# Forget gate as 16 more columns of the first keys' products, with later first heads and last pieces

## The chip, the cores and the metric

The kernel runs on one core of a Trainium2 chip. The metric is the device time of one execution in microseconds; three executions of the kernel before took 2311.81, 2313.56 and 2315.46 us, with a median of 2313.56 us.

The core has five engines that run side by side and wait for one another by semaphores: TensorE (PE, matrix products into PSUM), VectorE (DVE), ScalarE (ACT), GpSimd (POOL) and SyncE (SP). SP and POOL issue the transfers between HBM and the on-chip memory here. Each engine works through its own instructions in a fixed order.

## What is computed

Two decoder layers, D = 2048, 256 positions, float32. Layer 0 mixes with a gated MLP over positions and a linear recurrence, layer 1 with forgetting attention; after each comes a gated MLP with a short convolution. The change lies in the attention, `mixer_c`:

```python
def mixer_c(h, w_in, b_f, q_gain, k_gain, w_out):
    q, k, v, g, f = jnp.split(h @ w_in, [D_MODEL, 2 * D_MODEL, 3 * D_MODEL, 4 * D_MODEL], axis=-1)
    q = rms_norm(q.reshape(shp), q_gain)         # 16 heads of 128
    k = rms_norm(k.reshape(shp), k_gain)
    log_f = jax.nn.log_sigmoid(f + b_f)          # the forget gate: 16 columns, one for each head
    c = jnp.cumsum(log_f, axis=1).transpose(0, 2, 1)
    ...
        s = jnp.einsum('bthd,bshd->bhts', q[:, lo:hi], k[:, :hi]) * scale
        s = s + c[:, :, lo:hi, None] - c[:, :, None, :hi]
        p = jax.nn.softmax(jnp.where(causal, s, -jnp.inf), axis=-1)
    ...
    return (o * jax.nn.sigmoid(g)) @ w_out
```

The forget gate is a projection of the normed input onto only 16 columns, followed by a log-sigmoid and a running sum over the positions.

## The kernel before

Every projection is computed in float32 as three products of rounded parts. Activations and weights are split into a high part, rounded to the matrix engine's type (`ah`, `wh`), and the rest (`al`, `wl`); the products are `ah*wh + ah*wl + al*wh`. `weights()` does this for weights: SP loads a tile `w` from HBM (L156, four buffers), ACT casts it to `wh` (L162, three buffers), DVE subtracts to get `wl` (L165, three buffers), and PE multiplies. The three engines and SP form a pipeline that runs ahead of PE as far as the buffers allow.

`project_tok` (L194) computes one group of 512 columns (four heads) for all 256 positions. It runs over the 16 blocks of 128 rows of the weights (k = 0 to 15), two of them in each tile of 128x1024 (512 KB): a chunk. The two halves of the positions (T = 0, 1) have one PSUM bank each (the pool `pm`). Each chunk has 12 products of 512 columns (L225 to L227), each group 96. The norm's factor for a position is multiplied in when the bank is emptied, as the scale `Rt[:, T]` of an ACT instruction (L816).

In `mixer_c` the groups of heads are g = 0 to 3, each with queries Q, keys K and values V. Q0 and K0, those of the first group, are projected first (`early`); then the norm's finish makes the factors both for positions on partitions (`Rt`) and, by a product with a matrix of ones (`finish`, L353), for positions along the columns (`R`). Then for each group: Q and K are emptied, normed by head (L305, L306, L824), transposed in blocks of 32x32 by DVE (L250), and put in place by 16 copies from on-chip memory to on-chip memory (L255), eight of them issued by SP and eight by POOL. The results are the `turn` tiles. For g = 0 the forget gate stands ahead of V0's projection.

`forget()` (L728) projects with `w_cf`, whose 16 columns are padded to 128: two loads of 512 KB on SP and, for each k, one product of 512 columns with the high part of the weights stationary (L186: high and low part of the activations) and one of 256 with the low part (L189). The gate's columns end up on 128 partitions, positions along the columns. ACT and DVE fold the parts, multiply by `R`, add the bias and compute the log-sigmoid (L734 to L738), DVE scans over the positions (L739), and POOL writes the 16 rows to HBM (`cd`) and reads them back spread over all partitions (`cb`, 2 MB). `columns()` (L745) transposes `fc` on PE for the other direction (L748).

`attend(h, ...)` (L755) is one head's attention, written as a generator. `tick()` advances the generators in flight at every chunk, so that their pieces come between the chunks of later projections; at each `yield` a generator waits for the next `tick()`. Its first step casts the turned queries and keys to `qk` with their gains (L758); the next one computes the scores (L761, L762). `depth[0]` is how many generators run at a time, here two.

`add_four` (L367) and, in the `ffn` stage, `add_y` bring an output projection's piece q = 0 to 3 into the residual `x`: copy, transpose, 16 copies, then after `LAG` steps (one fewer for the last piece) four additions (L378) and the next norm's input; after the last piece and `WAIT` more steps comes the norm's `finish_tok`. `project_four` (L231, products L242 to L244) is the projection with weights from four blocks, used for the attention's gate, the output projections and the `ffn`.

The order of the instructions of each engine is set when the program is built: the program's order gives priorities, from which a scheduler places each engine's instructions, and generators interleave as said above. SP and POOL issue their transfers in their own order; each can be held up by a wait of the transfer at its head.

## Time and profile before

| What | Value |
|---|---|
| median of three runs | 2313.56 us |
| the runs | 2311.81, 2313.56, 2315.46 us |
| profiled execution, first to last instruction | 2312.9 us |
| mean granted clock of TensorE in it | 0.999 |
| PE busy | 2300.0 us, 99% |
| DVE busy | 1559.5 us, 67% |
| ACT busy | 1307.0 us, 57% |
| POOL busy | 350.4 us, 15% |
| DMA | 481.44 MB, 208 GB/s mean |

A row of the timeline reads: start in us from the beginning of the span, duration in us, engine, source line, operation, output and inputs by their names, shapes, number of instructions in the row, and in brackets the idle time of the engine ahead of it with what ended it. "SPq" and "POOL ... DMA_DIRECT2D" are the issues of transfers: their time is that of issuing, not that of the data. Durations of PE's products overlap, since the engine is pipelined: what a product costs is read from the distance between two starts. A row of the waits reads: the engine and the line that waited, the engine and the line that it waited for, microseconds in total, how often, the longest. A row of the groups reads: line, engine, operation, names, number | busy us, mean ns of one | idle us ahead of them, by releaser.

### The profile page before, as it was taken

How to read it: one execution, taken by the hardware profiler on the slowest of the kernel's cores; microseconds unless marked ns; L12 is line 12 of the kernel's file. 1: busy time of each engine (PE TensorE's matmuls, PEld its weight loads, DVE VectorE, ACT ScalarE, POOL GpSimd, SP SyncE). 2: the span in 40 equal slices, each digit the busy share in tenths (PEclk: the TensorE clock that was granted, in tenths of full speed). 3: DMA queues.
4: the chain of work that ended last, by engine and by line, in shares of the span. 5: the costliest groups of instructions: out<-in, count | busy, mean ns of one | idle time of the engine just before them, and what ended most of it. 6: DMA issues, size and time to landing. Idle time of an engine off the chain costs nothing.

```text
span 2312.9 us, 31358 instructions
## 1 busy us (share of the span) xinstructions
PE 2300.0 (99%) x10354; PEld 1904.7 (82%) x10354; DVE 1559.5 (67%) x2345; ACT 1307.0 (57%) x1958; POOL 350.4 (15%) x650
## 2 busy tenths in 40 slices
PE   9999999999999999999999999999999999999998
PEld 7888888888888888888888888887888888888887
DVE  7677866776566657766866665666776476667766
ACT  7567655665555546654565556655655465455642
POOL 0100112122012002111211101111221022012102
PEclk9999999999999999999999999999999999999999
DMA  8655577777677767776666655777777677667765
GB/s 274 204 161 173 175 218 220 235 235 212 208 210 207 217 196 212 223 216 186 197 230 194 190 182 178 225 221 227 225 219 216 192 218 209 210 205 213 222 206 166
DMA packets 497748, 481.44 MB, mean 208 GB/s; under 512 B 116288, under 2 KB 468688, under 8 KB 497456
## 3 DMA queue, kind: packets, MB, share of 16 engines
q1 hardware_dynamic: 475488, 453.08, 63.9%
q0 software_dynamic: 20944, 24.04, 4.5%
q10 hardware_dynamic: 1152, 2.31, 0.3%
q8 instruction: 81, 1.33, 0.3%
q14 instruction: 83, 0.68, 0.1%
HBM read 435.24 MB, written 2.11 MB: 189 GB/s over the span
## 4 chain that ended last, share of the span: by engine, by line
PE 95%; DVE 1%; DMA 1%; ACT 1%; issue 1%; POOL 0%; SPq 0%; ACTq 0%; DVEq 0%
PE pm L243 26%; PE pm L244 26%; PE pm L242 26%; PE pm L226 5%; PE pm L227 5%; PE pm L225 5%; DVE wl L165 1%; ACT wh L162 0%; PE px L593 0%; DMA w<-in_w_up 0%; PE pm L186 0%; DMA w<-in_w_v 0%; PE px L762 0%; DMA turn<-tmp 0%; PE px L784 0%
## 5 line engine op out<-in xcount | busy, mean ns | idle before, releaser
L165 DVE TENSOR_TENSOR wl<-w,wh 128x1024 fp32r<-128x1024 f32 (+1 forms) x820 | 998.5, 1220 | 647.2 <-ACT wh L162 639.1
L162 ACT ACTIVATE wh<-w 128x1024 fp32r<-128x1024 f32 (+1 forms) x820 | 864.1, 1056 | 797.2 <-PE pm L244 574.4
L242 PE MATMUL pm<-wh,a 128*128 128x512 f32 x1792 | 699.5, 391 | 1.5 <-ACT wh L162 1.5
L243 PE MATMUL pm<-wl,a 128*128 128x512 f32 x1792 | 699.1, 390 | 1.1 <-DVE wl L165 1.1
L244 PE MATMUL pm<-wh,a 128*128 128x512 f32 x1792 | 698.3, 390 | 0.0
L255 POOL DMA_DIRECT2D zt<-tmp x416 | 225.3, 550 | 1206.8 <-DVE tmp L250 1034.6
L243 PEld LDWEIGHTS pm<-wl,a 128*128 128x128 f32 x1792 | 337.0, 188 | 71.8 <-DVE wl L165 2.7
L242 PEld LDWEIGHTS pm<-wh,a 128*128 128x128 f32 x1792 | 336.7, 188 | 71.2 <-ACT wh L162 1.9
L244 PEld LDWEIGHTS pm<-wh,a 128*128 128x128 f32 x1792 | 336.9, 188 | 69.7
L242 PE MATMUL pm<-wh,hid 128*128 128x512 f32 x688 | 267.6, 389 | 0.0
L243 PE MATMUL pm<-wl,hid 128*128 128x512 f32 x688 | 267.6, 389 | 0.0
L244 PE MATMUL pm<-wh,hid 128*128 128x512 f32 x688 | 267.6, 389 | 0.0
L255 POOL DMA_DIRECT2D turn<-tmp x224 | 121.5, 550 | 739.5 <-DVE tmp L250 332.5
L225 PE MATMUL pm<-wh,a 128*128 128x512 f32 x504 | 199.2, 395 | 0.3 <-ACT wh L162 0.3
L226 PE MATMUL pm<-wl,a 128*128 128x512 f32 x504 | 196.5, 390 | 1.5 <-DVE wl L165 1.5
L227 PE MATMUL pm<-wh,a 128*128 128x512 f32 x504 | 196.5, 390 | 0.0
L244 PEld LDWEIGHTS pm<-wh,hid 128*128 128x128 f32 x688 | 129.1, 188 | 26.9
L243 PEld LDWEIGHTS pm<-wl,hid 128*128 128x128 f32 x688 | 129.1, 188 | 26.8
L242 PEld LDWEIGHTS pm<-wh,hid 128*128 128x128 f32 x688 | 129.1, 188 | 26.8
L226 PEld LDWEIGHTS pm<-wl,a 128*128 128x128 f32 x504 | 94.7, 188 | 21.3 <-DVE wl L165 2.1
L225 PEld LDWEIGHTS pm<-wh,a 128*128 128x128 f32 x504 | 94.7, 188 | 20.0 <-ACT wh L162 1.0
L227 PEld LDWEIGHTS pm<-wh,a 128*128 128x128 f32 x504 | 94.7, 188 | 19.8
(214 smaller groups left out, 1828.7 us busy)
## 6 DMA issues: line engine op xcount, KB each, us to landing
w<-in_w_up SPq DMA_DIRECT2D x352, 512.0 KB, 4.6
w<-in_w_dn SPq DMA_DIRECT2D x176, 512.0 KB, 4.5
w<-in_w_cqkv SPq DMA_DIRECT2D x96, 512.0 KB, 4.4
w<-in_w_abo SPq DMA_DIRECT2D x32, 512.0 KB, 4.8
w<-in_w_cg SPq DMA_DIRECT2D x32, 512.0 KB, 4.4
w<-in_w_co SPq DMA_DIRECT2D x32, 512.0 KB, 4.7
zt<-tmp SPq DMA_DIRECT2D x416, 32.0 KB, 2.8
zt<-tmp POOLq DMA_DIRECT2D x416, 32.0 KB, 2.6
```

What stands on the lines that cost most here:

```text
L162: deep["act"] = SC.activation(wh[:, p], w[:, p], AF.Copy)
L165: V.tensor_tensor(wl[:, p], w[:, p], wh[:, p].bitcast(F32), ALU.subtract)
L225: PE.matmul(ps[T], ah, h, start=k + i == 0, stop=False)
L226: PE.matmul(ps[T], ah, l, start=False, stop=False)
L227: PE.matmul(ps[T], al, h, start=False, stop=k + i == KT - 1)
L242: PE.matmul(ps[T], ah, h, start=k + i == 0, stop=False)
L243: PE.matmul(ps[T], ah, l, start=False, stop=False)
L244: deep['mm'] = PE.matmul(ps[T], al, h, start=False, stop=k + i == n - 1)
L255: (nc.sync, nc.gpsimd)[(a + b) % 2].dma_start(dst[BLK * b:BLK * (b + 1), :, a * n:(a + 1) * n], tmp[BLK * a:BLK * (a + 1), b * 4 * n:(b + ...
```

## The change

`w_cf`'s 16 columns go into K0's projection. For each k one tile of 528 columns is put together from two loads: 16 columns of `w_cf` (128 rows of 64 bytes, 8 KB, issued by POOL) and 512 columns of K's weights (256 KB, issued by SP). It is cast and split as one tile. Each of the 96 former products is two: one of 272 columns (the gate's 16 and K0's first 256) into a bank of the pool `px`, one of 256 columns into a bank of `pm`. K0's emptying takes four instructions for that reason.

The padded projection with its 1 MB of loads, the fold, and the factor `R` with its product are gone. `forget()` comes after K0's transposes in the program and ahead of V0's projection; it empties the 16 columns scaled by `Rt` (`ft`), transposes them on PE (two products into one bank), and goes on with 16 partitions in place of 128. `columns()` transposes 16 partitions in place of 128.

Three constants change. `STAND` is new: the first two heads of every group wait three steps more ahead of their first instruction. `LAST` = 5 replaces `LAG - 1` = 3 for the last piece of `add_four` and `add_y`; `WAIT` goes from 4 to 2. Helpers that are no longer called are removed.

The instructions in the order of each engine, before and after: PE 10021 and 10088 rows, DVE 2250 and 2250, ACT 1807 and 1811, POOL 94 and 110, SP 914 and 920. Around the end of K0 the order in the changed kernel is:

- SP: K0's sixteen loads, Q0's eight copies, V0's first six loads (chunks 0 to 5), K0's eight copies. Before, two loads of `w_cf` and V0's first two loads stood ahead of Q0's copies.
- POOL: sixteen loads of `w_cf`, Q0's eight copies, `cd`, `cb`, K0's eight copies. Before: Q0's, K0's, `cd`, `cb`.
- ACT: the casts of K0's last tiles, the emptying of K0 and the gate, two `qk` casts of queries, the gate's Abs, the cast of V0's first tile, the gate's Exp and Ln with the head norm's between, the next casts of V0.
- PE: K0's last product, the two transposes of the gate, V0's first chunk; the transposes of `columns()` in V0's third chunk.

With `LAST` and `WAIT` the order of every engine at the ends of the first three stages stays as it was; the very last addition of the program moves.

```diff
 LAG = 4
-WAIT = 4
+LAST = 5
+WAIT = 2
+STAND = 3
...
-        early = project_tok(w_cqkv[0], norm), project_tok(w_cqkv[CH // 4], norm)
+        first = project_tok(w_cqkv[0], norm)
+        pa, pb = [bank() for _ in range(2)], [pm.tile([P, 512], F32, tag="pm", name=nm("pm")) for _ in range(2)]
+        n = CH + 512
+        for k in range(KT):
+            if k % 2 == 0:
+                tick()
+            w = wp.tile([P, n], F32, tag="w", name=nm("w"), bufs=4)
+            wh = wp.tile([P, n], F32R, tag="wh", name=nm("wh"), bufs=3)
+            wl = wp.tile([P, n], F32R, tag="wl", name=nm("wl"), bufs=3)
+            nc.gpsimd.dma_start(w[:, 0:CH], w_cf[:, k * P:k * P + CH])
+            nc.sync.dma_start(w[:, CH:n], w_cqkv[CH // 4][:, k * 512:(k + 1) * 512])
+            deep["act"] = SC.activation(wh, w, AF.Copy)
+            V.tensor_tensor(wl, w, wh.bitcast(F32), ALU.subtract)
+            a = norm.a[k]
+            for T in range(2):
+                ah, al = a[:, T * P:(T + 1) * P], a[:, S + T * P:S + (T + 1) * P]
+                for j, (a_, t) in enumerate(((ah, wh), (ah, wl), (al, wh))):
+                    start, stop = k + j == 0, k == KT - 1 and j == 2
+                    PE.matmul(pa[T][:, 0:CH + S], a_, t[:, 0:CH + S], start=start, stop=stop)
+                    PE.matmul(pb[T][:, 0:S], a_, t[:, CH + S:n], start=start, stop=stop)
         drain()
         depth[0] = 2
-        R, Rt = norm.finish(), norm.Rt
+        Rt = norm.Rt
...
         def forget():
-            f = project_norm(w_cf, A, R, hp.tile([P, S], F32, tag="f", name="f"))
+            f = hp.tile([P, S], F32, tag="f", name="f")[0:CH]
+            ft = hp.tile([P, 2, LANE], F32, tag="ft", name="ft")
+            ps = bank()
+            for T in range(2):
+                SC.activation(ft[:, T, 0:CH], pa[T][:, 0:CH], AF.Copy, scale=Rt[:, T:T + 1])
+                PE.transpose(ps[0:CH, T * P:(T + 1) * P], ft[:, T, 0:CH], ident)
...
-            V.tensor_scalar(f, f, pp[:, C_BF:C_BF + 1], None, ALU.add)
+            V.tensor_scalar(f, ps[0:CH, 0:S], pp[0:CH, C_BF:C_BF + 1], None, ALU.add)
...
         def columns(fc):
             ps = bank()
             for T in range(2):
-                PE.transpose(ps[:, T * P:(T + 1) * P], fc[:, T * P:(T + 1) * P], ident)
+                PE.transpose(ps[:, T * CH:(T + 1) * CH], fc[:, T * P:(T + 1) * P], ident[0:CH, 0:CH])
...
         def attend(h, q, k, v, o):
             d0 = (h % 4) * P
+            for _ in range(STAND if h % 4 < 2 else 0):
+                yield
...
             for j in range(3):
-                if g == 0 and j == 2:
-                    fc = forget()
-                ps = early[j] if g == 0 and j < 2 else project_tok(w_cqkv[j * (CH // 4) + g], norm)
+                ps = None if g == 0 and j == 1 else first if g + j == 0 else \
+                    project_tok(w_cqkv[j * (CH // 4) + g], norm)
                 z = piece("z", 2) if j < 2 else piece("v", 2)
                 for T in range(2):
-                    SC.activation(z[:, T], ps[T], AF.Copy, scale=Rt[:, T:T + 1])
+                    if ps is None:
+                        SC.activation(z[:, T, 0:S], pa[T][:, CH:CH + S], AF.Copy, scale=Rt[:, T:T + 1])
+                        SC.activation(z[:, T, S:512], pb[T][:, 0:S], AF.Copy, scale=Rt[:, T:T + 1])
+                    else:
+                        SC.activation(z[:, T], ps[T], AF.Copy, scale=Rt[:, T:T + 1])
...
                 qkv.append(z)
+                if g == 0 and j == 1:
+                    fc = forget()
...
     def add_four(q, ps, z, tmp, dst, nxt):
...
-            for _ in range(LAG - (q == 3)):
+            for _ in range(LAST if q == 3 else LAG):
                 yield
...
         def add_y(q, finish):
...
-                for _ in range(LAG - (q == 3)):
+                for _ in range(LAST if q == 3 else LAG):
                     yield
```

More of the change, by code (lines that the diff above doesn't have):

```diff
@@ L257, in transposed @@
                                   .rearrange("p (m r) -> p m r", m=4))
-    def fold(ps):
-        t = tp.tile([P, S], F32, tag="ev", name=nm("ev"), bufs=3)
-        SC.activation(t, ps[:, S:2 * S], AF.Copy)
-        V.tensor_tensor(t, ps[:, 0:S], t, ALU.add)
-        return t
-    def project_norm(wsrc, acts, R, out=None, run=2):
-        t = fold(project(wsrc, acts, run=run))
-        if out is None:
-            out = t
-        V.tensor_tensor(out, t, R, ALU.mult)
-        return out
     def split(dst, src, gain=None, eng=SC, turn=False):
@@ L349, in finish_tok @@
             self.Rt = Rt
-        def finish(self, tok=False):
-            ps = bank()
-            PE.matmul(ps[:, 0:S], ones, self.acc, start=True, stop=True)
-            R = cp.tile([P, S], F32, tag="R", name=nm("R"), bufs=2)
-            rsq(R, ps[:, 0:S], D)
-            if not tok:
-                return R
-            for _ in self.finish_tok():
-                pass
-            return R, self.Rt
-    def add_x(m, ps):
-        t = tp.tile([P, S], F32, tag="ev", name=nm("ev"), bufs=3)
-        SC.activation(t, ps[:, S:2 * S], AF.Copy)
-        V.tensor_tensor(xT[m], xT[m], ps[:, 0:S], ALU.add)
-        V.tensor_tensor(xT[m], xT[m], t, ALU.add)
     def add_four(q, ps, z, tmp, dst, nxt):
@@ L740, in forget @@
             cd = dp.tile([CH, S], F32, tag="cd", name="cd")
-            nc.gpsimd.dma_start(cd, fc[0:CH, :])
+            nc.gpsimd.dma_start(cd, fc)
             nc.gpsimd.dma_start(cb, cd.partition_broadcast(P))
```

10 lines of the change are left out of this document (5 added, 5 removed).

## The prediction

> **What bounds the kernel now.** I read the page first: the span, the busy shares, the chain of work that ended last.
>
> ```profile
> span 2312.9 us, 31358 instructions
> PE 2300.0 (99%) x10354; PEld 1904.7 (82%) x10354; DVE 1559.5 (67%) x2345; ACT 1307.0 (57%) x1958; POOL 350.4 (15%) x650
> PE 95%; DVE 1%; DMA 1%; ACT 1%; issue 1%; POOL 0%; SPq 0%; ACTq 0%; DVEq 0%
> ```
>
> PE is 95% of the chain. A change can therefore save time in two ways only: fewer or shorter products, or less waiting by PE. It can lose by making PE wait. The table of waits for PE says how little waiting there is:
>
> ```profile
> PE pm L226 <- DVE wl L165: 1.5, 2, 0.8
> PE pm L242 <- ACT wh L162: 1.5, 1, 1.5
> ```
>
> Then the timeline of PE at the place that the change touches: the end of K0 (the first keys), R's product, the forget gate, the start of V0.
>
> ```profile
> 1155.88 0.39 PE L227 MATMUL pm<-wh,a 128*128 128x512 f32 x1
> 1156.10 0.59 PE L353 MATMUL px<-acc,ones 128*128 128x256 f32 x2
> ...
> 1157.25 0.62 PE L186 MATMUL pm<-a,wh 128*128 128x512 f32 x2
> 1157.94 0.63 PE L186 MATMUL pm<-a,wh 128*128 128x512 f32 x2
> ...
> 1162.12 0.40 PE L225 MATMUL pm<-wh,a 128*128 128x512 f32 x1
> ```
>
> K0 ends at 1156.10 and V0 starts at 1162.12 with no idle time marked between. Those 6.02 us are PE work that the change takes out. What else they do is seen on SP's queue and on ACT in the same stretch:
>
> ```profile
> 1142.87 2.78 SPq L156 DMA_DIRECT2D w<-in_w_cf  x2
> 1147.77 3.27 SPq L156 DMA_DIRECT2D w<-in_w_cqkv  x2
> 1151.97 5.37 SPq L255 DMA_DIRECT2D turn<-tmp  x8
> 1157.75 4.36 SPq L156 DMA_DIRECT2D w<-in_w_cqkv  x4
> ```
>
> The two loads at 1147.77 are V0's first, issued ahead of Q0's eight turned copies; the two `w_cf` loads stand ahead of them. So before the change, PE had the forget weights and two V loads in hand while SP spent 5.37 us on copies.
>
> **The change part by part.** *Forget products out, wider K0 products in.* R's product and the 16 + 16 forget products go: 1162.12 - 1156.10 = 6.02 us off PE. K0's 96 products of 512 columns become 96 of 272 and 96 of 256. A 512-column product costs 1156.10 - 1155.88 = 0.22, over longer runs 0.227 us. Two of 512 with two of 256 take 1157.94 - 1157.25 = 0.69, so one of 256 is (0.693 - 0.453) / 2 = 0.120. I take 0.127 for 272 (sixteen columns more at (0.227 - 0.120) / 256 each). Per old product: 0.127 + 0.120 - 0.227 = +0.020, times 96 = +1.9 us. Bounds: 0 if the split were free, +3 if the rows' rounding (0.01) falls against it. K0 then ends at E = 1156.1 + 1.9 = 1158.0. Of this sum the Trainium skill ("TensorE: Matmul & The Clock Gate", Back-to-back issue gap) has another price: a gap of N/2.4 + 2.5 ns, so a split costs about 9 ns and the 96 of them an estimated 0.9 us, a result 1 us lower; the rows' spacing of 227 ns for 512 columns is over its 216, and I go by the rows.
>
> *Transposes.* Two of the gate's 128x16 tiles are added behind K0; the two in V's third chunk shrink:
>
> ```profile
> 1183.91 0.38 PE L748 MATMUL px<-cst,fc 128*128 128x128 f32 x2
> ```
>
> About 0.2 us net; 0 to 0.5.
>
> *What stands ahead of V0 now.* Program order on SP becomes K0's sixteen 256 KB loads, Q0's eight copies, then V0's load: no load of V is ahead of the copies, and there is no PE work behind K0 to cover them. On ACT, between K0's evacuation and the cast of V0 (`wh`, L162), stand two `qk` casts (L758), which need all sixteen of Q0's copies, and the Abs of the gate (L735). Whatever holds `qk` holds these, and with V0's cast DVE's `wl` and all of PE. The sixteen `w_cf` loads on POOL wait for the same `w` buffers as SP's, so the last goes out near 1149.5, ahead of Q0's copies; they hold nothing up there. In before the two steps on ACT were:
>
> ```profile
> 1160.27 0.50 ACT L758 ACTIVATE qk<-turn,gq 128x256 f32<-128x256 f32 x1
> ...
> 1168.76 0.40 ACT L735 ACTIVATE fa<-f 128x256 f32<-128x256 f32 x1
> ...
> 1174.21 1.06 ACT L162 ACTIVATE wh<-w 128x1024 fp32r<-128x1024 f32 x1 [1.29 <-DMA w<-in_w_cqkv]
> ```
>
> DVE has Q0's transposes at 1150.60 and ends them at 1151.9:
>
> ```profile
> 1150.60 1.30 DVE L250 STREAM_TRANSPOSE tmp<-z 128x512 f32<-128x512 f32 x2
> ```
>
> Q0 itself is unchanged, so this stays near 1151.5. SP's copies then run 1151.6 to 1156.8 (5.2 us), and V0's load goes out at 1156.9. After K0's copies a load issued at 1170.37 was cast at 1174.21, 3.84 us later:
>
> ```profile
> 1165.15 5.11 SPq L255 DMA_DIRECT2D turn<-tmp  x8
> 1170.37 1.48 SPq L156 DMA_DIRECT2D w<-in_w_cqkv  x3
> ```
>
> So V0's `wh` starts at 1160.7 at the earliest, E + 2.7; with 1 us more for a later landing E + 3.7. Add the cast, 1.06: first V product at E + 3.8 to 4.8. The `wl` product behind it waits for DVE (L165), 0.8 as in the waits above, and after such a pause PE loses clock or waits once more: 1.4 us, worked out below. Together 6.0 to 7.0 us of loss behind E if nothing else is late.
>
> *POOL's pause.* POOL issues the other eight copies of each batch. In the timeline of POOL, a pause of some 2.1 to 2.4 us with the releaser "issue" recurs inside a batch:
>
> ```profile
> 858.77 0.55 POOL L255 DMA_DIRECT2D zt<-tmp  x1 [2.09 <-issue]
> ...
> 1152.56 4.33 POOL L255 DMA_DIRECT2D turn<-tmp  x8 [33.99 <-DMA w<-in_w_cqkv]
> ...
> 1223.11 4.37 POOL L255 DMA_DIRECT2D turn<-tmp  x8 [45.41 <-issue]
> ...
> 1585.33 1.63 POOL L255 DMA_DIRECT2D turn<-tmp  x3 [17.42 <-DVE tmp L250]
> 1589.35 2.71 POOL L255 DMA_DIRECT2D turn<-tmp  x5 [2.39 <-issue]
> ```
>
> The groups of POOL's DMAs between the pause at 858 and that at 1221, then between 1222 and 1588, give 89 + 16 + 1 + 1 = 107 and 107:
>
> ```profile
> L255 POOL DMA_DIRECT2D zt<-tmp x89 | 48.2, 550 | 213.7 <-DVE tmp L250 132.3 <-issue 81.4
> L255 POOL DMA_DIRECT2D turn<-tmp x16 | 8.7, 550 | 42.5 <-DMA w<-in_w_cqkv 34.0 <-DVE tmp L250 8.5
> L742 POOL DMA_DIRECT2D cb<-cd x1 | 0.6, 575 | 5.0 <-DMA cd<-fc 5.0
> L741 POOL DMA_DIRECT2D cd<-fc x1 | 0.5, 511 | 1.9 <-DVE fc L739 1.9
> ...
> L255 POOL DMA_DIRECT2D turn<-tmp x107 | 58.0, 550 | 351.2 <-DVE tmp L250 144.3 <-ACT wh L162 106.0 <-issue 100.9
> ```
>
> One DMA counts as one, small `cd` and large `cb` alike. The change puts sixteen more on POOL (one `w_cf` load of 8 KB for each k) ahead of Q0's copies. Before, Q0's and K0's sixteen copies, `cd` and `cb` lay between the count and the pause ahead of Q1's first copy; sixteen more DMAs bring that pause forward to about Q0's third copy (18 - 16 = 2 behind its first). The pause 107 further on moves from q = 3 of the output projection (fourth copy, 1589.35) to q = 1 of it.
>
> In before the pauses at Q1 and at q = 3 are where PE waited:
>
> ```profile
> 1235.47 0.50 PE L225 MATMUL pm<-wh,a 128*128 128x512 f32 x1 [0.29 <-ACT wh L162]
> 1236.73 0.50 PE L226 MATMUL pm<-wl,a 128*128 128x512 f32 x1 [0.76 <-DVE wl L165]
> ...
> 1599.59 0.39 PE L244 MATMUL pm<-wh,a 128*128 128x512 f32 x1
> 1601.45 0.50 PE L242 MATMUL pm<-wh,a 128*128 128x512 f32 x1 [1.48 <-ACT wh L162]
> 1602.71 0.50 PE L243 MATMUL pm<-wl,a 128*128 128x512 f32 x1 [0.76 <-DVE wl L165]
> ...
> 1604.01 0.63 PE L242 MATMUL pm<-wh,a 128*128 128x512 f32 x1
> ...
> 1607.00 0.55 PE L243 MATMUL pm<-wl,a 128*128 128x512 f32 x1
> ```
>
> At Q1 the step from L225 to L226 is 1.26 instead of 0.23, the wait ahead of it 0.29; with the edges 1.6 us. At q = 3 the step to 1601.45 is 1.86 instead of 0.23, the next 1.26 instead of 0.23, and from 1604.01 to 1607.00 seven steps take 2.99 instead of 1.59: 1.6 + 1.0 + 1.4, with the edges 4.4 us. The Trainium skill (the same page, Part 1) has the clock fall to half after an idle window of about 3.4 us; the rows show nearly twice the spacing after two gaps of 1.6 and 1.0, and by either a wait of 8 us here is followed by slow products.
>
> With the pause in Q0's copies POOL ends them late. Before, it began 0.59 behind SP (1152.56) and took 4.33; now it would begin at 1152.2 and end at 1152.2 + 4.33 + 2.4 = 1158.9. How long after that the copies are used: at most 3.4 us without a pause (1156.89 to the `qk` at 1160.27, which waited for no DMA); 6.05 at Q1 (1227.48 to the row below) and 5.6 at q = 3 (1592.06 to the row below), where SP's next loads ran at the same time:
>
> ```profile
> 1233.53 0.93 ACT L758 ACTIVATE qk<-turn,gq 128x256 f32<-128x256 f32 x2 [5.42 <-DMA w<-in_w_cqkv]
> ...
> 1597.70 1.10 DVE L378 TENSOR_TENSOR x<-x,turn 128x256 f32<-128x256 f32 x3 [3.53 <-DMA w<-in_w_up]
> ```
>
> V0's loads follow Q0's copies in the same way, so I go by the upper rows and take 5.2, a little less, since K0's last `w` buffers come free one by one: `qk` at 1164.1 = E + 6.1, bounds E + 4.3 and E + 6.95. Then 0.9 for two of them, 0.40 for the Abs, 1.06 for the cast: first V product at E + 8.4; `wl` 0.8 and clock 1.4 make it 10.6, bounds 8.8 and 11.5.
>
> *STAND, LAST, WAIT.* STAND moves the scores of a group's first two heads by three chunks; work of the same size, later, between products that are ready: 0, with -1 to +1 for a cover missed. LAST and WAIT leave the order of every engine at the three norm boundaries as it was and move only the very last addition: 0.
>
> *Sum*, against the profiled 2312.9: -6.0 + 1.9 + 0.2 + 10.6 - 1.6 (no pause in Q1) = +5.1, with nothing for the pause moved from q = 3 to q = 1, where the additions meet the same burst of loads (-4.4 to +0.6). Span 2318.0; the median of the runs, 2313.56, lies 0.66 above the profile, so 2318.7.
>
> **The rivals.**
>
> *No pause at Q0.* If what POOL counts is not DMAs (descriptors, instructions), the pause falls among the `w_cf` loads, 5 us ahead of need. Then only V0's load behind the copies is left: -6.0 + 1.9 + 0.2 + 6.5 - 1.6 = +1.0, about 2314.6, with 2313 to 2316. For: `w_cf` has 128 rows of 64 bytes, a shape that no row of before shows. Against: the two 107s with `cb` in one.
>
> *Covered.* V0's cast isn't held: the copies land in 2 us as their normal median, ACT takes `qk` before E, V0's first product comes within 2 us of E, and PE's two old waits vanish. -6.0 + 1.9 + 0.2 + 3 - 1.6 - 4.4 = -6.9, about 2306.7. For: before's `qk` at 1160.27 waited for no DMA, though SP's copies had ended at 1157.34. Against: SP's queue, where V0's load cannot pass the copies.
>
> *K0 starves.* Four buffers of one k hold half the prefetch of four of two: 4 x 6 x 0.247 = 5.9 us against 4 x 12 x 0.227 = 10.9, with two small DMAs per k, one on POOL with its 2 us pauses. If one k comes late, PE waits 1 to 4 us and the clock falls (1.4): 2 to 5 more, 2320 to 2324 along with the forecast's boundary. The Trainium skill ("DMA: Bandwidth & Descriptors", Specifications) speaks for it: rows under 512 B are slow, and these are 64 B; no row of before has one.
>
> *Edits without effect.* That LAST and WAIT do nothing is in the sum; 0 either way.
>
> **How the numbers follow.** Forecast 42% (2318.7, own range 2316 to 2321); no pause at Q0 27%; covered 18%; starved 13%. A change of 0.2%, 4.6 us, is about what a measurement tells from none. The forecast lies at +5.1, so part of it counts as the same; of the pause moved to q = 1 some fall to either side. Slower: 28 of the forecast's 42 and 12 of starved, 40%. Faster: the covered 18 and 6 of the others with q = 3's 4.4 us gone, 24%. Same 36%. The range 2307 to 2322 leaves out the far ends of covered and starved.
>
> **What would show it.** L353 and L186 gone, K0's products at 0.247 a pair. PE idle behind the last of them: `wh` of V0 waiting on `qk`, and `qk` on the turned copies; a POOL pause inside Q0's batch and none at Q1; products at twice the spacing after it. I am wrong if the gap on PE between K0 and V0 is under 5 us, if POOL's pause lies elsewhere, or if K0's products wait.

## The result and the profile after

| | before | after |
|---|---|---|
| median of six runs each, side by side | 2314.57 us (2311.81 to 2318.26) | 2325.18 us (2319.48 to 2329.15) |
| ratio of the two, 95% interval | | 1.0044 [1.0034, 1.0055] |
| profiled execution, span | 2312.9 us | 2327.3 us |

The changed kernel is slower by 10.6 us in the medians, where +5.1 was forecast; the time of 2318.7 is 6.5 us too low. The profiled execution of after is the slowest of its six runs (2329.15 us), so its trace shows more loss than the medians: 14.4 us of span.

The page of after begins like this: the span, the busy times, the shares of the chain that ended last.

```profile
span 2327.3 us, 31551 instructions
PE 2301.9 (99%) x10418; PEld 1907.1 (82%) x10418; DVE 1554.8 (67%) x2345; ACT 1306.5 (56%) x1965; POOL 358.8 (15%) x666
PE 93%; DMA 2%; DVE 1%; ACT 1%; issue 1%; SPq 0%; POOL 0%; ACTq 0%; DVEq 0%; POOLq 0%
```

PE's busy time is only 1.9 us higher, and its share of the chain fell from 95% to 93%: the loss is mostly waiting. The table of PE's waits (engine and line that waited, what it waited for, us in total, how often, the longest) says for what:

```profile
PE pm L227 <- ACT wh L164: 9.9, 2, 7.1
PE pm L228 <- DVE wl L167: 2.9, 3, 1.7
```

To see where each microsecond came in, I set the start of every product that both kernels have against its start in before. This lag grows or shrinks at the places in the table and is flat between them, but for short swings where `STAND` has moved pieces of heads:

| place in the profiled executions | change of the lag | forecast |
|---|---|---|
| ahead of the attention, at 33 and 460 us | +2.5 | none |
| K0, and on to the steady part of V0 | +6.7 | -6.0 + 1.9 + 0.2 + 10.6 = +6.7 |
| V0's seventh tile | +5.4 | no such term |
| rest of g = 0, small steps | -0.4 | 0 |
| Q1 | -1.4 | -1.6 |
| output projection, q = 1 and q = 3 | +6.35 and -4.4 | 0 together |

The sum is +14.75. The first line is not the change's: one `wl` came late at 33 us (1.7 of the 2.9 us in the table of waits), and a small step follows at 460 us. The work up to K0 is the same in the kernels below, and just ahead of K0 their profiled executions lag by -0.5 to +6.1 us (b1, b2 and c2, which have wider buffers, left out). The rest is the change: 12.3 us in this execution, 10.6 us between the medians.

The place behind K0, in the timeline of PE: the gate's columns in K0's last products, its first transpose, V0's first products.

```profile
1156.25 0.30 PE L707 MATMUL px<-wl,a 128*128 128x272 f32 x1
...
1157.73 0.30 PE L707 MATMUL px<-wl,a 128*128 128x272 f32 x1
...
1160.34 0.27 PE L708 MATMUL pm<-wh,a 128*128 128x256 f32 x1
1161.73 0.28 PE L725 MATMUL px<-cst,ft 128*16 128x128 f32 x1 [0.62 <-ACT ft L724]
1169.09 1.22 PE L227 MATMUL pm<-wh,a 128*128 128x512 f32 x2 [7.08 <-ACT wh L164]
...
1170.94 0.63 PE L229 MATMUL pm<-wh,a 128*128 128x512 f32 x1
...
1172.22 0.54 PE L229 MATMUL pm<-wh,a 128*128 128x512 f32 x1
...
1173.75 0.40 PE L227 MATMUL pm<-wh,a 128*128 128x512 f32 x1
```

Six pairs of 272 and 256 columns take 1157.73 - 1156.25 = 1.48 us, 0.247 a pair. K0's last product starts at 1160.34, the next projection's first at 1169.09; behind it, three steps take 1172.22 - 1170.94 = 1.28, 0.43 each instead of 0.23. The granted clock of PE is 0.57 of full speed from 1165 to 1170 us and 0.75 from 1170 to 1175. The last row is the start of V0's second tile. K0 ends at 1160.34 + 0.12 = 1160.46, with 0.12 for its last product of 256 columns, and the first tile's twelve products take 12 x 0.227 = 2.72. So 1173.75 - 1160.46 - 2.72 = 10.6 us are lost behind K0. The same stretch on ACT, POOL and SP:

```profile
1166.85 0.94 ACT L756 ACTIVATE qk<-turn,gq 128x256 f32<-128x256 f32 x2 [5.17 <-DMA w<-in_w_cqkv]
...
1167.99 1.04 ACT L164 ACTIVATE wh<-w 128x1024 fp32r<-128x1024 f32 x1
```
```profile
1153.78 0.56 POOL L257 DMA_DIRECT2D turn<-tmp  x1 [1.02 <-DVE wl L701]
1156.88 3.80 POOL L257 DMA_DIRECT2D turn<-tmp  x7 [2.53 <-issue]
...
1175.38 0.57 POOL L738 DMA_DIRECT2D cb<-cd  x1 [3.18 <-DMA cd<-fc]
...
1186.35 0.55 POOL L257 DMA_DIRECT2D turn<-tmp  x1 [6.57 <-DMA cb<-cd]
```
```profile
1158.92 14.03 SPq L158 DMA_DIRECT2D w<-in_w_cqkv  x6
1175.04 5.84 SPq L257 DMA_DIRECT2D turn<-tmp  x8
1180.98 17.59 SPq L158 DMA_DIRECT2D w<-in_w_cqkv  x8
```

On POOL the pause, 2.53 us, sits behind the first of Q0's copies. The eighth copy goes out at 1160.68 and `qk` starts at 1166.85; the cast of V0 stands behind two `qk` and the Abs. Further down the same queue stands what the forecast passed over: `cd`, then `cb`, the spread of 2 MB, and only then K0's copies; ahead of the last of them POOL is idle for 6.57 us, until `cb` has landed. SP's eight copies of K0 went out meanwhile, and right behind them the load of V0's seventh tile, at 1180.98. PE and ACT at that tile:

```profile
1190.78 0.73 PE L227 MATMUL pm<-wh,a 128*128 128x512 f32 x2 [2.79 <-ACT wh L164]
1192.04 0.50 PE L228 MATMUL pm<-wl,a 128*128 128x512 f32 x1 [0.53 <-DVE wl L167]
1189.67 1.06 ACT L164 ACTIVATE wh<-w 128x1024 fp32r<-128x1024 f32 x1 [8.74 <-DMA w<-in_w_cqkv]
```

The load issued at 1180.98 was cast at 1189.67, 8.7 us later, against 3.84 in before; ACT had been waiting for it. Slow products follow here too: the granted clock is 0.80 from 1190 to 1195 us. Last, q = 1 of the output projection, POOL first and then PE:

```profile
1558.48 3.25 POOL L257 DMA_DIRECT2D turn<-tmp  x6 [2.46 <-issue]
1569.19 0.39 PE L246 MATMUL pm<-wh,yc 128*128 128x512 f32 x1
1571.95 0.79 PE L244 MATMUL pm<-wh,yc 128*128 128x512 f32 x1 [2.37 <-ACT wh L164]
1573.21 0.80 PE L245 MATMUL pm<-wl,yc 128*128 128x512 f32 x1 [0.46 <-DVE wl L167]
...
1578.49 0.51 PE L245 MATMUL pm<-wl,yc 128*128 128x512 f32 x1
```

The steps are 2.76 and 1.26 us instead of 0.23 each, then twelve steps take 5.28 instead of 12 x 0.227 = 2.72: 2.5 + 1.0 + 2.6 = 6.1 us, where q = 3 of before lost 4.4.

### The profile page after: what moved, and what is told of

It reads as the page before. It is cut to its first block, busy times and chain, and to the rows that moved or that the text cites. A ratio compares the mean times of both kernels' runs of the same rounds, so it can differ in the third digit from the quotient of the medians.

```text
span 2327.3 us, 31551 instructions
## 1 busy us (share of the span) xinstructions
PE 2301.9 (99%) x10418; PEld 1907.1 (82%) x10418; DVE 1554.8 (67%) x2345; ACT 1306.5 (56%) x1965; POOL 358.8 (15%) x666
## 4 chain that ended last, share of the span: by engine, by line
PE 93%; DMA 2%; DVE 1%; ACT 1%; issue 1%; SPq 0%; POOL 0%; ACTq 0%; DVEq 0%; POOLq 0%
PE pm L245 25%; PE pm L246 25%; PE pm L244 25%; PE pm L228 4%; PE pm L229 4%; PE pm L227 4%; DMA w<-in_w_up 1%; DMA w<-in_w_cqkv 1%; ACT wh L164 1%; DVE wl L167 1%; PE px L565 0%; DMA wt<-in_spw 0%; DMA w<-in_w_v 0%; PE px L707 0%; PE pm L708 0%
## 5 line engine op out<-in xcount | busy, mean ns | idle before, releaser
L167 DVE TENSOR_TENSOR wl<-w,wh 128x1024 fp32r<-128x1024 f32 (+1 forms) x810 | 986.3, 1221 | 653.6 <-ACT wh L164 633.6
L164 ACT ACTIVATE wh<-w 128x1024 fp32r<-128x1024 f32 (+1 forms) x810 | 853.2, 1056 | 790.0 <-PE pm L246 566.0
L245 PE MATMUL pm<-wl,a 128*128 128x512 f32 x1792 | 698.4, 390 | 0.5 <-DVE wl L167 0.5
L244 PE MATMUL pm<-wh,a 128*128 128x512 f32 x1792 | 698.7, 390 | 0.0
L246 PE MATMUL pm<-wh,a 128*128 128x512 f32 x1792 | 697.8, 389 | 0.0
L245 PEld LDWEIGHTS pm<-wl,a 128*128 128x128 f32 x1792 | 336.6, 188 | 70.7 <-DVE wl L167 1.7
L246 PEld LDWEIGHTS pm<-wh,a 128*128 128x128 f32 x1792 | 336.5, 188 | 69.6
L244 PEld LDWEIGHTS pm<-wh,a 128*128 128x128 f32 x1792 | 336.4, 188 | 69.3
L246 PE MATMUL pm<-wh,hid 128*128 128x512 f32 x688 | 267.6, 389 | 0.0
L227 PE MATMUL pm<-wh,a 128*128 128x512 f32 x472 | 187.7, 399 | 9.9 <-ACT wh L164 9.9
L228 PE MATMUL pm<-wl,a 128*128 128x512 f32 x472 | 186.3, 395 | 3.0 <-DVE wl L167 2.9
L229 PE MATMUL pm<-wh,a 128*128 128x512 f32 x472 | 185.2, 392 | 0.0
L246 PEld LDWEIGHTS pm<-wh,hid 128*128 128x128 f32 x688 | 129.1, 188 | 26.7
L227 PEld LDWEIGHTS pm<-wh,a 128*128 128x128 f32 x472 | 89.1, 189 | 28.7 <-ACT wh L164 10.8
L913 ACT ACTIVATE conv<-zt,pp 128x256 f32<-128x256 f32 x176 | 95.4, 589 | 25.4 <-DMA zt<-tmp 24.0
L228 PEld LDWEIGHTS pm<-wl,a 128*128 128x128 f32 x472 | 89.5, 190 | 23.3 <-DVE wl L167 4.9
```

What stands on the lines that cost most here:

```text
L164: deep["act"] = SC.activation(wh[:, p], w[:, p], AF.Copy)
L167: V.tensor_tensor(wl[:, p], w[:, p], wh[:, p].bitcast(F32), ALU.subtract)
L227: PE.matmul(ps[T], ah, h, start=k + i == 0, stop=False)
L228: PE.matmul(ps[T], ah, l, start=False, stop=False)
L229: PE.matmul(ps[T], al, h, start=False, stop=k + i == KT - 1)
L244: PE.matmul(ps[T], ah, h, start=k + i == 0, stop=False)
```

## The experiments

Each time is a median, with that of the kernel before in the same session beside it. Differences "to before" are of these; after is +10.6. "Order" in a diff makes an instruction stand behind another one on its queue and nothing else.

| kernel | median, before | ratio [95%] | to before |
|---|---|---|---|
| a1_cb_late | 2319.92, 2313.95 | 1.0021 [1.0012, 1.0030] | +6.0 |
| a2_cf_act | 2318.79, 2313.95 | 1.0022 [1.0013, 1.0031] | +4.8 |
| a3_before_knobs | 2315.63, 2313.95 | 1.0007 [0.9998, 1.0016] | +1.7 |
| a4_before_16 | 2312.23, 2313.95 | 0.9996 [0.9988, 1.0005] | -1.7 |
| b1_two_k | 2335.20, 2315.00 | 1.0086 [1.0072, 1.0100] | +20.2 |
| b2_two_k_cb | 2332.89, 2315.00 | 1.0072 [1.0060, 1.0085] | +17.9 |
| b3_cf_cb | 2316.97, 2315.00 | 1.0010 [1.0001, 1.0019] | +2.0 |
| b4_qk_late | 2317.78, 2315.00 | 1.0010 [1.0001, 1.0019] | +2.8 |
| c2_after_1056 | 2343.90, 2314.32 | 1.0127 [1.0114, 1.0140] | +29.6 |
| d1_ahead | 2314.18, 2314.32 | 1.0000 [0.9992, 1.0009] | -0.1 |
| d2_ahead3 | 2315.23, 2314.32 | 1.0006 [0.9997, 1.0015] | +0.9 |
| d3_ahead_act | 2315.78, 2314.32 | 1.0008 [0.9999, 1.0016] | +1.5 |
| f1_cb_behind | 2320.96, 2314.40 | 1.0030 [1.0018, 1.0041] | +6.6 |
| e1_best | 2315.04, 2314.40 | 1.0004 [0.9994, 1.0013] | +0.6 |
| e2_best_act | 2317.35, 2314.40 | 1.0012 [1.0003, 1.0021] | +3.0 |
| e3_later | 2311.44, 2314.49 | 0.9986 [0.9977, 0.9995] | -3.1 |

The ratio is not the quotient of the two medians: for a1 it stands for +4.9 us instead of +6.0. So differences of about 1 us between two kernels are not to be read.

**The spread later (a1).** After, with the scan, `cd` and `cb` emitted behind V0's projection (from here on "..." marks lines left out of a diff):

```diff
-            V.tensor_tensor_scan(fc, on, f, 0.0, ALU.mult, ALU.add)
...
+            r = V.tensor_tensor_scan(fc, on, f, 0.0, ALU.mult, ALU.add)
+            tc.add_manual_dep(r.ins, deep["wl"][-2].ins.name, order, reason="late")
```

> The changed kernel with one thing moved: the gate's scan, and with it the 2 MB spread of its sums, comes after the sixth chunk of V0 on DVE, and K0's copies stand ahead of it on POOL. Theory (the second stall, 1187.6 to 1190.8, is V's seventh load slowed by the spread's traffic and by K0's copies just ahead of it on SP): the 5.4 us of that place go, everything else stays: 5 to 5.5 us under the changed kernel, some 2319.5. Rival (SP's eight copies alone hold that load): the wait shrinks by 1.5 us at most. Rival (the spread, late, holds the scores instead): a new wait on DVE at the first scores, no gain.

PE's wait at V0's seventh tile is gone and that behind K0 stays, in a1's table of waits:

```profile
PE pm L228 <- ACT wh L164: 6.7, 1, 6.7
```

The lag there grows by some 5.2 us less than in after, and the median is 4.6 us lower. So the stall comes from `cd` and `cb` being where they are; by what path, f1 tries below.

**The loads of `w_cf` off POOL (a2).** After, with one word changed:

```diff
-            nc.gpsimd.dma_start(w[:, 0:CH], w_cf[:, k * P:k * P + CH])
+            nc.scalar.dma_start(w[:, 0:CH], w_cf[:, k * P:k * P + CH])
```

> The changed kernel with its sixteen small loads of the gate's weights issued by ACT in place of POOL, so that POOL's count of transfers is that of the kernel before. Theory (POOL pauses after every 107 transfers, whatever their size): no pause in Q0's copies, pauses again ahead of Q1's first copy and at the fourth piece of the output projection, none at its second. The wait behind K0 shrinks from 7.1 to 2 to 4 us, Q1's 1.4 to 1.6 us come back, the output projection's 6.3 become 4.4: 4 to 6 us under the changed kernel, 2319 to 2321. Rival (V0's load behind SP's copies sets the wait, not POOL): the wait behind K0 stays within 1 us of 7.1, and only 0.5 us are gained.

The timeline of a2, POOL and PE:

```profile
1151.35 4.34 POOL L257 DMA_DIRECT2D turn<-tmp  x8 [32.63 <-DVE wl L701]
1157.96 0.27 PE L708 MATMUL pm<-wh,a 128*128 128x256 f32 x1
1161.60 1.22 PE L227 MATMUL pm<-wh,a 128*128 128x512 f32 x2 [1.96 <-ACT wh L164]
...
1167.25 0.39 PE L227 MATMUL pm<-wh,a 128*128 128x512 f32 x1
```

Eight copies without a pause, and V0's first product 3.6 us behind K0's last instead of 8.75. V0's second tile starts at 1167.25, which by the same sum is a loss of 6.4 us behind K0, where after has 10.6. The pauses were back at Q1 and at q = 3. The sixteen DMAs on POOL move the pause, as the count of 107 says.

**The constants alone (a3)**: `STAND`, `LAST` and `WAIT` put into before, nothing else.

```diff
-WAIT = 4
+LAST = 5
+WAIT = 2
+STAND = 3
...
```

> The kernel before with the three constants alone (first two heads of a group three steps later, last piece 5, wait 2). Theory: the same as before within 1 us, 2314, since PE has products ready in each place where heads move. Rival (the constants are what costs): slower by 2 us or more; rival (they were the gain, hidden by the rest): faster by 2 us or more, the first heads no longer waiting for the spread sums.

The interval holds 1; in the profile the lag at the end is 0.03 us. They cost nothing that can be told.

**The count alone (a4)**: before, with sixteen loads of 8 KB that nobody reads, on POOL during K0.

```diff
...
+            for i in range(c):
+                nc.gpsimd.dma_start(extra(k + i), w_cf[:, (k + i) * P:(k + i) * P + CH])
...
```

> The kernel before with sixteen loads of 8 KB added on POOL during K0, into a tile that nothing reads, the gate's padded projection kept. Theory (count of transfers): the pause moves from Q1's batch into Q0's and from the output projection's fourth piece to its second, as in the changed kernel; Q1's 1.6 us of waiting go, the output projection's 4.4 become some 6; Q0's copies land 2 to 4 us later, under the gate's products: 0 to +3 us, 2314 to 2317. Rival (the pause isn't counted in transfers): the pauses stay where they are, and so does the time.

The timeline of a4 shows both pauses where after has them, and what q = 1 then cost on PE:

```profile
1154.79 3.81 POOL L258 DMA_DIRECT2D turn<-tmp  x7 [2.53 <-issue]
1544.71 3.26 POOL L258 DMA_DIRECT2D turn<-tmp  x6 [2.45 <-issue]
1557.52 0.50 PE L245 MATMUL pm<-wh,yc 128*128 128x512 f32 x1 [1.72 <-ACT wh L162]
```

So the place of the pause depends on the number of DMAs and not on their use. The lag changed by +1.9 at Q0, -1.5 at Q1, +3.0 at q = 1 and -4.4 at q = 3; with small steps that makes -1.5, near the medians' -1.7, where I had expected 0 to +3. Behind Q0, with the forget products still there as cover, the same pause costs 1.9 us; the price at q = 1 is not fixed: 3.0 here, 6.35 in after.

**Tiles of two k for K0 (b1, b2)**: sixteen tiles become eight of 1056 columns, `w_cf` on ACT's queue; b2 adds a1's edit.

```diff
-            w = wp.tile([P, n], F32, tag="w", name=nm("w"), bufs=4)
...
+            w = wp.tile([P, 2 * n], F32, tag="w", name=nm("w"), bufs=4)
...
```

> The changed kernel with K0's tiles of two k instead of one (1056 columns, eight loads of 512 KB on SP; the gate's columns in eight small loads issued by ACT). On SP three loads of V0 then stand ahead of Q0's copies, and on ACT two casts of V0 ahead of K0's emptying. Theory (what costs behind K0 is that the tiles of one k halve what is loaded ahead, so that V0's load comes behind the copies): no wait of PE behind K0 over 1.5 us; with 6.0 us of products gone and 2.1 added 3 to 4 us under the kernel before, 2310 to 2311. Rival (the gate's chain through ACT and its transposes hold V0 in any case): the wait stays 4 us or more, 2316 or more.

> The kernel of tiles of two k with the 2 MB spread of the gate's sums moved behind V0's sixth chunk as well. Theory: with V's loads in hand early the spread's traffic delays nothing that PE waits for, so within 1.5 us of the kernel of tiles of two k alone. Rival (the spread costs wherever it meets loads): 2 to 5 us better or, late, worse through the first scores.

The gap behind K0 closes, as b1's timeline shows:

```profile
1167.75 0.28 PE L713 MATMUL pm<-wh,a 128*128 128x256 f32 x1
...
1167.89 0.47 PE L227 MATMUL pm<-wh,a 128*128 128x512 f32 x1
```

Yet b1 is slower than after by 10 us: its lag is already 10.2 us ahead of K0, where the code is unchanged. Many products have become a little slower. I had foreseen nothing of the kind, and made c2 for it.

**The width of the buffers alone (c2)**: after, with the weight buffers 1056 columns wide instead of 1024, of which 1024 are used.

```diff
-        w = pool.tile([P, n], F32, tag="w", name=nm("w"), bufs=nw)
...
+        w = pool.tile([P, WIDE if pool is wp and n == 1024 else n], F32, tag="w", name=nm("w"), bufs=nw)[:, 0:n]
...
```

> The changed kernel with nothing moved but the width of the weight tiles' buffers, 1056 columns in place of 1024, of which the same 1024 or 528 are used: the control for the kernels of two k, whose products took 228 to 232 ns in place of 227 throughout. Theory (where the operands lie sets the time of a product): the same slower products in every stage, 15 to 20 us over the changed kernel, 2340 to 2345. Rival (the wider tiles' loads or casts cost it): the products stay at 227 ns and the time at 2325.

It is 19.0 us slower than after. One group of products, out of after's page and then out of c2's:

```profile
L245 PE MATMUL pm<-wl,a 128*128 128x512 f32 x1792 | 698.4, 390 | 0.5 <-DVE wl L167 0.5
```
```profile
L246 PE MATMUL pm<-wl,a 128*128 128x512 f32 x1792 | 703.2, 392 | 0.0
```

The same 1792 products, with next to no wait ahead of them, take 4.8 us more of busy time. The third product of each step (`al*wh`, the groups of after's L246 and c2's L247) grows by only 1.6 of 697.8 us, so not every product pays. So b1 and b2 say nothing about tiles of two k by themselves: their 18 to 20 us hide a boundary that is 4.4 us better than before's. (b2 is 2.3 us faster than b1, more than the 1.5 expected.) What in the placement slows a product wasn't tried.

**Q0's `qk` later on ACT (b4)**: after, the two `qk` of the first heads ordered behind V0's third cast.

```diff
+                if h < 2:
+                    tc.add_manual_dep(r.ins, deep["wh3"].ins.name, order, reason="late")
```

> The changed kernel with the two query casts of the first heads behind V0's third cast on ACT. Theory (V0's first cast, its load long landed, is held by these casts, which wait for POOL's last copies): V0's first product comes 3 to 4 us earlier, at E + 4 to 5, and 2321 to 2322. Rival (V0's load, slow among the copies, is the hold): 0 to 1 us. Rival (V's later stall takes it back): the gap behind K0 shrinks but the one in V grows, total within 1 us of 2325.

The timeline of b4, one row of ACT and three of PE:

```profile
1159.98 1.06 ACT L164 ACTIVATE wh<-w 128x1024 fp32r<-128x1024 f32 x1
1157.33 0.27 PE L713 MATMUL pm<-wh,a 128*128 128x256 f32 x1
...
1161.09 0.73 PE L231 MATMUL pm<-wh,a 128*128 128x512 f32 x2 [2.08 <-ACT wh L164]
...
1166.25 0.48 PE L231 MATMUL pm<-wh,a 128*128 128x512 f32 x1
```

The pause is still in POOL's batch and SP's copies still stand ahead of V0's load. V0's second tile starts at 1166.25, so 1166.25 - 1157.45 - 2.72 = 6.1 us are lost behind K0, 4.5 less than in after. So it was the order on ACT that carried POOL's pause to PE. What is left is the larger part, and it goes with V0's load behind SP's copies: that load was issued at 1155.85 and landed 4.0 us later, just as its cast began. The stall at V0's seventh tile, 4.3 us, stays, as it should. In all b4 gained more than the 3 to 4 us expected.

**Both cures (b3)**, a1's and a2's edits together:

> The changed kernel with both earlier edits: the gate's loads issued by ACT and the spread behind V0's sixth chunk. Theory (the spread's traffic and the place of the pause are separate costs, the second stall partly follows from the first): 1 to 2 us under the kernel with the loads on ACT alone, 2317 to 2318; not 5 us, since there the stall in V was only some 1.4 us. Rival (the two add in full): 2313.5.

It stands 8.6 us under after, as expected (2317 to 2318); a1 and a2 alone gain 4.6 and 5.8, which add up to more.

**K0's copies ahead of the spread (f1)**: after, with `cd` ordered behind the last of K0's copies on POOL.

```diff
-            nc.gpsimd.dma_start(cd, fc)
+            r = nc.gpsimd.dma_start(cd, fc)
+            tc.add_manual_dep(r.ins, deep["pcopy"].ins.name, order, reason="behind")
```

> The changed kernel with one order changed: on POOL K0's copies stand ahead of the gate's two transfers (16 KB out, 2 MB back), whose source is ready as early as before. Theory (the traffic of the 2 MB spread makes V's seventh load late): the spread now starts some 5 us later, beside that load's end and the next ones; 2 to 5 us of the 5.4 stay, 2322 to 2325. Rival (the order on POOL, K0's last copy waiting for the spread, is the cause): all of it goes as with the late scan, some 2320.

The stall at V0's seventh tile is gone entirely; my expectation that 2 to 5 us of it stay was wrong. The table of DMA issues between 1160 and 1200 us (output and input, queue, number, KB each, median us from issue to landing), for before, after and f1 in this order:

```profile
turn<-tmp SPq DMA_DIRECT2D x8, 32.0 KB, 2.1
```
```profile
cb<-cd POOLq DMA_DIRECT2D x1, 2048.0 KB, 10.7
turn<-tmp SPq DMA_DIRECT2D x8, 32.0 KB, 10.2
```
```profile
turn<-tmp SPq DMA_DIRECT2D x8, 32.0 KB, 2.2
```

SP's copies do not stand in POOL's order, and yet they landed after 10.2 us with the spread issued among them and after 2.2 with it behind. The load of V0's seventh tile, which SP issued right behind its copies without a wait for POOL, landed after 8.6 us in after. So what holds PE here is the traffic of the spread, and POOL's order acts by setting when the spread starts. Loads behind the spread are as late in the other kernels: in before the one issued at 1178.3 landed after 10.7 us, in f1 the one at 1179.7 after 10.5. But there the seventh and eighth loads of V0 had gone out ahead of it, and PE did not have to wait.

**Other orders, to close the gap (d1 to d3, e1 to e3).** d1: V0's first two loads ahead of Q0's copies on SP, with a1's and b4's edits; d2: three loads; d3: d1 with a2's edit. e1: three loads ahead of Q0's copies and eight ahead of K0's, `qk`, the Abs, the transposes and the first scores each behind work of V0 that is ready earlier, the scan behind V0's fifth `wl`; e2: e1 with a2's edit; e3: e1 with K0's head norm, Q0's `qk` and the Abs one tile later still. The first lines are d1's against after, the others e3's against e1.

```diff
+                    for r in deep["q0"]:
+                        tc.add_manual_dep(r.ins, deep["loads"][1].ins.name, order, reason="queue order")
...
-                        tc.add_manual_dep(r.ins, deep["wl"][2].ins.name, order, reason="late")
+                        tc.add_manual_dep(r.ins, deep["wl"][3].ins.name, order, reason="late")
+                    tc.add_manual_dep(deep["rsq"].ins, deep["seen"][3].ins.name, order, reason="late")
...
```

> The changed kernel, same tiles and same transfers on the same queues, in another order: on SP two loads of V0 ahead of Q0's copies, on ACT the two query casts behind V0's third cast, and the 2 MB spread behind V0's sixth chunk. Theory (all that the change lost behind K0 and in V0 is order, the products saved are real): first product of V0 within 1 us of K0's end; against the kernel before -6.0 + 2.1 = -3.9 there, -1.5 at Q1, -4.4 + 2.9 to 6.3 at the output projection: -2 to -7, 2307 to 2313. Rival (the waits only move, to V0's third load behind the copies or to the paused copies): 2 us or more of waiting in V0 and 2314 or more.

> As the reordered kernel with two loads ahead, with three loads of V0 ahead of Q0's copies. Theory: the same within 1.5 us, since the third load is needed 5.4 us after V0's start and comes in time in both. Rival (with two ahead the third load is late): 1 to 3 us better than with two. Rival (the copies, later by one load, hold the query casts and V's fourth cast): 1 to 4 us worse.

> As the reordered kernel with two loads ahead, with the gate's sixteen loads issued by ACT, so that POOL pauses at Q1 and at the output projection's third or fourth piece as in the kernel before. Theory (the place of the pauses is worth what PE waits there): Q1's 1.5 us come back, the output projection waits 4.4 in place of 2.9 to 6.3, Q0 nothing in both: within 3 us of the reordered kernel, more likely above it. Rival (issuing on ACT costs ACT time that PE waits for): 3 us or more above it, with waits of PE inside K0.

> The changed kernel in a new order from K0's end through V0: three loads of V0 ahead of Q0's copies and all eight ahead of K0's on SP; on ACT Q0's casts behind V0's third cast, the gate's steps behind the fourth, K0's casts behind the eighth; on DVE K0's head norm behind V0's third tile, the scan behind the fifth; on PE the gate's transposes behind V0's second chunk, the first scores behind Q1's fourth chunk as in the changed kernel. Theory (the saving is real and only covered by waits of order): -3.9 at K0 with under 1.5 us of waits in V0, -1.5 at Q1, +0.5 to +2 at the output projection: 2309 to 2311, 3 to 5 us under the kernel before. Rival (something in V0 waits still): 2313 to 2316, with the wait on PE named in V0 or Q1.

> As the kernel in the new order, with the gate's sixteen small loads issued by ACT, so that POOL pauses where it did before the change. Theory: Q1's 1.5 us come back, the output projection costs what it did before: within 2 us of the kernel in the new order, 2309 to 2312. Rival (ACT's issuing delays the casts of K0): waits of PE inside K0, 3 us or more above it.

> As the kernel in the new order, with K0's head norm (its two steps on ACT, its scaling and transposes on DVE) and Q0's casts one tile of V0 further back. Theory (DVE's work for K0, some 5 us without any product to cover it now, is what V0's tiles wait for): the waits for DVE in V0 shrink from 3.5 to 4.5 us to 1 to 2.5, and the time to 2312 to 2314. Rival (V0's fourth load, behind Q0's copies on SP, is late by itself): the same waits, now for ACT's cast, and 2315.

d1's timeline shows the gap closed, and where part of it went:

```profile
1158.23 0.28 PE L717 MATMUL pm<-wh,a 128*128 128x256 f32 x1
1158.34 0.39 PE L233 MATMUL pm<-wh,a 128*128 128x512 f32 x1
...
1168.47 0.50 PE L234 MATMUL pm<-wl,a 128*128 128x512 f32 x1 [2.57 <-DVE wl L173]
```

The lag is -4.3 at V0's start, which is the part of the change that was to be gained: -6.0 + 1.9 and the edges. Then the gate's transposes wait 0.99 us for ACT, and ten microseconds later DVE, busy with K0's norm and transposes, is late with a `wl` by 2.57: the gain is given back, as d1's rival had it. The intervals of d1, d2 and d3 hold 1; d2's profiled execution lost 5.5 us at 460 us, in work that is unchanged, and is no guide. e1 has nearly the same -4.2, then waits of 2.1 us for DVE in V0, and -0.8 is left at V0's end, so it misses the expected 2309 to 2311; e2, expected within 2 us of e1, has the pause back at Q1 and q = 3 and is slower than e1 by 2.3. e3 moves DVE's norm off the casts:

```profile
1157.72 0.28 PE L717 MATMUL pm<-wh,a 128*128 128x256 f32 x1
1157.84 0.39 PE L233 MATMUL pm<-wh,a 128*128 128x512 f32 x1
PE pm L234 <- DVE wl L173: 1.3, 2, 0.8
```

The last row is from e3's table of waits over the whole program; 0.5 of its 1.3 us lies in V0. Of the -4.2 at V0's start -2.9 outlasts V0, Q1 makes it -4.5, q = 1 and q = 3 of the output projection give +6.2 and -4.4, and the end is at -2.7. By its median e3 is 3.1 us under before and 13.7 under after, the best of all kernels here.

## Why the prediction was wrong

**Forget products out, wider products in: right.** Where the start was undisturbed, K0's last product starts at 1157.96 (a2) and 1157.72 (e3), so K0 ends 0.12 later, at 1157.8 to 1158.1; forecast 1158.0. A pair takes 0.247, as taken. By the Trainium skill ("TensorE: Matmul & The Clock Gate", Back-to-back issue gap) K0 would have ended an estimated 1 us earlier; the trace goes with the rows.

**Transposes: no weight.** They lie in the gap (1161.73), which other things set.

**Behind K0: right in mechanism and in size.** The pause is in Q0's batch, behind the first copy where the third was forecast. From POOL's last copy to `qk` it is 1166.85 - 1160.68 = 6.17 (taken 5.2, bounded by 6.05), and from K0's end at 1160.46 to V0's first product 8.63 (forecast 8.4). Products at twice the spacing follow, as forecast. The loss behind K0 is 10.6, the forecast's figure. That it fits to the tenth is luck: `qk` came 6.4 behind K0's end instead of 6.1, and what followed V0's first product cost 1.9 instead of 2.2. The floor for V0's load behind SP's copies, "6.0 to 7.0 us of loss behind E", holds as well: b4 leaves that load where it is and loses 6.1, a2, without the pause, 6.4. The order on ACT, which held V0's cast for POOL's pause, carried the rest.

**The count: right.** a4 and a2 put the pauses at Q0 and q = 1, or back at Q1 and q = 3, by sixteen DMAs more or less on POOL. Q1 gave 1.4 back, forecast 1.6.

**The constants: right**, zero in a3.

**The missing term: "What stands ahead of V0 now" ended with V0's first cast.** The listed orders of the queues had it: on POOL `cd` and `cb` ahead of K0's copies, where before they were behind, and on SP K0's copies and then V0's seventh load, as before, but now with the spread in flight. The forecast costed moves ahead of V0 and gave those inside V0 no price. They cost 5.4 us in the profile; a1 and f1, each of which removes that stall alone, are 4.6 and 4.0 us nearer to before than after is.

**"Nothing for the pause moved from q = 3 to q = 1": mis-sized.** The bounds were -4.4 to +0.6; measured in after's profile were +6.35 and -4.4, +1.95 together, outside them. In a4 it was +3.0 and -4.4, inside them. The waits differ less than that, 2.37 and 0.46 us in after, 1.72 and 0.76 in a4; the rest is PE's clock. Two rows for the stretch from 1540 to 1600 us, after and then a4 (length, busy time of PE, its weight loads, DVE, ACT and POOL, granted clock of PE, share and GB/s of the DMA):

```profile
1540.00:1600.00 60.00, 57.16 (x239) 46.40 (x238) 39.50 (x59) 31.32 (x48) 8.67 (x16) 0.94 0.66 200
```
```profile
1540.00:1600.00 60.00, 57.53 (x253) 47.06 (x252) 39.73 (x59) 31.90 (x48) 13.04 (x24) 1.00 0.70 212
```

0.06 x 60 is some 3.6 us of clock that after lost and a4 did not. The other kernels with the pause at q = 1 fall in line: where the granted clock of ten microseconds around the waits is 1.00, the price is 2.6 to 3.1 us (a1, a4, b4, f1), at 0.83 it is 4.7 to 5.5 (d1, d2, e1), at 0.66 it is 6.2 to 6.35 (after, e3). Why the clock fell in some of these executions and not in others stays open. The forecast had priced slow products behind K0 and at q = 3, and none at q = 1.

With the two, 5.4 + 1.95 = 7.35 and the smaller errors -0.2, the forecast's +5.1 would be +12.25; without the 2.5 us of the start that is the profile's lag. The median's +10.6 is 1.6 lower, within the scatter of after's own runs (9.7 us); with a4's +3.0 at q = 1 the sum would be +8.9, so the median lies between the two. The stated range ended at 2322 because no rival held a stall inside V0.

**The rivals.** *K0 starves* is false: in the groups of after between 1140 and 1160.7 us K0's products have no idle time ahead of them; one row of the four:

```profile
L707 PE MATMUL px<-wh,a 128*128 128x272 f32 x56 | 15.2, 294 | 0.0
```

The 64-byte rows, which by the Trainium skill ("DMA: Bandwidth & Descriptors", Specifications) are too short for line rate, cost PE no wait here. *No pause at Q0* is a2, at +4.8 instead of the rival's +1.0: behind K0 it loses 6.4 where the rival took 6.5, but Q1's pause is back (1.6 that the rival had taken off) and a small stall in V0 remains. *Covered* is false in after. d1 and e3 show what it takes: V's loads ahead of the copies on SP, and `qk` behind V0's casts on ACT.

## What to carry to other kernels

When work that covered something is taken out, follow every queue past the next cast, up to the first place where PE again runs on tiles that were loaded well ahead: here the larger surprise lay thirty microseconds behind the edit, in an order of transfers that was written down and not priced. Ask which load is issued behind a large transfer, on whatever queue. A few small transfers added to a queue can shift a periodic pause of that queue by hundreds of microseconds, so count them and look where the pause lands, and give each landing place a price with a wide range. A saving on the engine that bounds the kernel arrives only if the other engines' work is re-ordered for it: of 4.1 us of saved products after kept none, and e3 2.9 as far as V0's end.

## What the runs showed of the hardware

- GpSimd's issue of transfers pauses for 2.1 to 2.5 us (before, after, a4) at a place that moves with the number of its transfers: sixteen of only 8 KB moved both pauses (a4), and taking them away moved both back (a2).
- The place or pitch of the weight buffers alone changes the time of many products: 1056 instead of 1024 columns made the kernel 19.0 us slower (c2), about 0.8%.
- A 2 MB spread in flight raises the time to landing of 32 KB copies issued on another queue from 2.2 to 10.2 us (f1, after), and that of a 512 KB load from 3.8 (before) to 8.6 (after).
- Two waits of PE at one place (q = 1), 2.5 us together in a4 and 2.8 in after, cost 3.0 us in a4, where the granted clock stayed at 1.00, and 6.35 in after, where it was 0.66 over the ten microseconds around them.
